# A hybrid decoder trunk: the attention gate on GpSimd, and each recurrent head's result turned one step later

## The chip, the cores and the metric

One core of a Trainium2 chip runs the whole program. The metric is device time in microseconds (us) of one execution; lower is better. The engines are TensorE (PE; its weight loads are listed as PEld), VectorE (DVE), ScalarE (ACT), GpSimd (POOL) and the queue of SyncE (SP). Each engine works through its own list of instructions in order and waits on semaphores; ACT, POOL and SP also issue DMAs.

## What is computed

Two layers over 1024 tokens of width 1024. Each layer normalises, projects, and runs two token mixers side by side: sliding-window attention and a gated linear recurrence (HGRN2). Both results are gated, projected up, merged, projected out and added to the input. Cut to what matters here:

```python
for layer in range(DEPTH):                       # 2
    h = rms_norm(x, norm_w[layer])
    (q, k, v, z_attn, q_h, f_h, i_h, g_h, gate_attn, gate_hgrn) = split(h @ w_in[layer])
    ...
    a = sliding_window_attention(q, k, v, sinks) * silu(z_attn)        # the gate of attention
    ...
    o = hgrn2_recurrence(heads(qin), heads(kin), heads(i_h), heads(logf))   # 4 heads of 128
    o = o * rsqrt(mean(o * o) + eps) * hgrn_norm_w[layer]
    b = o.reshape(B, T, 512) * silu(g_h)
    merged = sigmoid(gate_attn) * (a @ w_up_attn) + sigmoid(gate_hgrn) * (b @ w_up_hgrn)
    x = x + merged @ w_out[layer]
return rms_norm(x, final_norm_w)
```

All of it is float32. To keep that precision, the large products are made from operands that are each split into two parts of a narrower matmul type (fp32r): a high part, cast by ScalarE, and a low part, which is the operand less its high part. Three matmuls (low x high, high x low, high x high) stand for one.

## The kernel before

Tiles have 128 partitions. The names that matter:

- `slot(...)` hands out one of 39 SBUF buffers of 128 x 1024 floats; a load into a slot waits until the last reader of its former content is done. `bank(...)` hands out one of five PSUM banks, `pj` three more.
- `split_slot` (line 380) splits an operand: `S.copy` casts the high part on ScalarE (line 383), a subtraction makes the low part (line 384). `split_w` (136, 137) does the same for weights.
- `colsA` and `up` issue the projections, three matmuls a term through `proj3` (147 to 149).

The stage of a layer that the change touches is the heads. After attention, the four heads of the recurrence run as generators `core(h)` of ten steps each, one head started every five steps of a loop over `t`. A head's steps are these. Steps 0 and 1 load `f`, `R`, `Q` from DRAM (SP queue) and multiply them up on VectorE (`grow`, lines 946, 955, 958, and 967 to 975). Step 2 makes the first small score matmuls (`lv`, 933 and 992), which wait for those products. Steps 3 to 5 grow further, and step 6 makes the next score matmuls (`l`, `lv_m`, 1044 to 1057) and, in the step behind it, the masked scores are copied into `scT`, four pieces by GpSimd (1070). Then comes a turn of `R` (`tn`, 1080), and the state products (`kv`, 1092), which VectorE chains from chunk to chunk (1096, 1098). The last step makes the head's outputs (`po`, 1109 and 1111), copies them (1112) and sums their squares on ScalarE (1114), computes the reciprocal root on VectorE in small instructions (`ms_o`, lines 116 to 130) and scales the result (`tab`, 1116).

`finish_head` (1117 on) then turns the head's result: a load of its gate (`gg`, 1119), eight PE transposes (`tb`, 1125), a VectorE product with the norm's gain and the gate (`b`, 1126) and, for every second head, a split.

So that TensorE is not idle while a head's chain runs on other engines, the loop takes pieces of "filling" from a second generator: twelve halves of the projections of heads 1 to 3 (24 matmuls each; DVE subtracts the low part of their weights at line 137), then the up-projections of attention (`up_attn`, tiles `pu_ua`; 12, 12 and 24 matmuls a piece, twelve pieces). Between these, at the four pieces of `GATE = (6, 7, 8, 9)`, `gate_attn` loads a quarter of attention's output (`ar<-ad`) and of its gate (`zr<-zd`), multiplies them (line 1140) and splits the product (383, 384). The up-projections of attention read these splits; those of the recurrence (`pu_uh`), after the loop, read the splits of `b`.

The order within each engine's list is not simply the program's: the framework orders instructions when the program is built, by its own estimate of when each can start; where several can, the earlier in the program goes first. On the chip each list is then followed in that order.

## Time and profile before

| | |
|---|---|
| median of three runs | 1387.02 us (1384.45 to 1387.6) |
| the profiled execution | 1387.23 us, of which 1385.5 us lie between its first and last instruction |
| mean granted clock of TensorE | 0.996 |
| busy: PE, PEld, DVE, ACT, POOL | 98%, 81%, 72%, 51%, 8% of the span |
| the heads' stage | about 425 to 575 us in layer 0, 1119 to 1256 us in layer 1 |
| gate products (line 1140) | 8 on DVE, 1.22 us each |
| their low parts (line 384, `wl_a`) | 8 on DVE, 1.22 us each |
| the whole of POOL's other copies into `scT` | 32, 0.66 us each |

A row of the timeline gives start and duration in us, the engine, the line, the operation, the tiles (written <- read), shapes and count, and in brackets how long the engine idled before it and what released it. A row of waits gives who waited for whom, the total in us, how often, and the longest. A matmul of 512 columns is listed with 0.39 us because matmuls overlap; one starts every 0.23 us.

### The profile page before, as it was taken

The numbers are of one execution on the slowest core, as the hardware profiler recorded it, in microseconds if no ns is written. First come the engines' busy times: TensorE is split into PE (matmuls) and PEld (weight loads), VectorE is DVE, ScalarE is ACT, GpSimd is POOL, SyncE is SP. The second block draws the span as 40 slices with busy tenths as digits, with TensorE's granted clock in tenths as the row PEclk, the third lists the DMA queues.
The fourth block names the chain that finished last, engine by engine and source line by source line (L and its number), as shares of the span: only waits on it lengthen the run. The fifth ranks groups of instructions, "written<-read, shape, count | busy, mean of one in ns | idle before, by whom it ended". The sixth has DMA issues, their size and how long they took to land.

```text
span 1385.5 us, 21538 instructions
## 1 busy us (share of the span) xinstructions
PE 1356.9 (98%) x8236; PEld 1127.0 (81%) x8236; DVE 997.3 (72%) x1638; ACT 708.8 (51%) x1418; POOL 109.2 (8%) x195
## 2 busy tenths in 40 slices
PE   7999999999999999999999999999999999999997
PEld 7888888888877888888888888887887788788885
DVE  6867668843646898599959666776356487867998
ACT  8844333443786655323666333344367766352254
POOL 1100012320000001000000001222100000100000
PEclk9999999999999999999999999999999999999999
DMA  9444476875225652860256336587913476329203
GB/s 290 165 134 145 137 225 204 264 262 212 92 95 189 231 189 76 310 239 29 86 181 189 126 125 194 173 259 217 335 49 107 142 236 217 108 85 402 91 1 122
DMA packets 204279, 240.06 MB, mean 173 GB/s; under 512 B 14288, under 2 KB 140752, under 8 KB 204176
## 3 DMA queue, kind: packets, MB, share of 16 engines
q1 hardware_dynamic: 156528, 145.08, 32.0%
q10 hardware_dynamic: 34944, 52.44, 10.4%
q0 software_dynamic: 12704, 41.17, 9.3%
q8 instruction: 65, 1.06, 0.3%
q14 instruction: 38, 0.31, 0.1%
HBM read 160.00 MB, written 78.64 MB: 172 GB/s over the span
## 4 chain that ended last, share of the span: by engine, by line
PE 80%; DVE 13%; ACT 3%; DMA 2%; issue 2%; SPq 0%; DVEq 0%; ACTq 0%
PE pb L308 6%; PE pb L310 6%; PE pb L309 6%; PE pc L308 4%; PE pc L310 4%; PE pc L309 4%; PE pg L270 3%; PE pg L272 3%; PE pg L271 3%; PE pu_uh L149 2%; PE pu_uh L147 2%; PE pu_uh L148 2%; PE pi L843 2%; PE pi L842 2%; PE pi L844 2%; PE av L816 2%
## 5 line engine op out<-in xcount | busy, mean ns | idle before, releaser
L136 ACT CAST whi_s<-ws 128x1024 fp32r<-128x1024 f32 x30 | 31.6, 1054 | 90.4 <-PE pc L310 89.0
L319 DVE TENSOR_TENSOR pq<-pc,pq 128x512 f32<-128x512 f32 x37 | 25.6, 691 | 61.4 <-PE pc L310 56.2
L136 ACT CAST whi_o<-wo 128x1024 fp32r<-128x1024 f32 x20 | 21.1, 1054 | 78.7 <-PE pu_uh L149 35.5
L544 ACT ACTIVATE pq<-pq 128x512 f32<-128x512 f32 x60 | 37.9, 631 | 43.9 <-DVE pq L319 42.3
L136 ACT CAST whi_t<-ws 128x1024 fp32r<-128x1024 f32 x30 | 31.6, 1054 | 41.8 <-PE pc L310 27.9
L147 PE MATMUL pu_ua<-wh_a,wlo_ua 128*128 128x512 f32 x128 | 52.2, 408 | 0.0
L780 ACT ACTIVATE pr<-pr,mx 128x128 f32<-128x128 f32 x128 | 49.6, 391 | 4.1 <-DVE mx L777 3.7
L149 PE MATMUL pu_ua<-wh_a,whi_ua 128*128 128x512 f32 x128 | 51.0, 399 | 0.0
L148 PE MATMUL pu_ua<-wl_a,whi_ua 128*128 128x512 f32 x128 | 50.3, 393 | 0.0
L147 PE MATMUL pu_uh<-wh_b,wlo_uh 128*128 128x512 f32 x128 | 49.8, 389 | 0.0
L148 PE MATMUL pu_uh<-wl_b,whi_uh 128*128 128x512 f32 x128 | 49.8, 389 | 0.0
L149 PE MATMUL pu_uh<-wh_b,whi_uh 128*128 128x512 f32 x128 | 49.8, 389 | 0.0
L270 PE MATMUL pg<-hh,wl_p 128*128 128x512 f32 (+1 forms) x128 | 46.9, 368 | 1.0 <-DVE wl_p L384 1.0
L308 PE MATMUL pb<-th,wl 128*128 128x512 f32 x120 | 47.2, 393 | 0.5 <-ACT pq L349 0.4
L308 PE MATMUL pb<-th,wlo_s 128*128 128x512 f32 x120 | 47.1, 392 | 0.0
L308 PE MATMUL pc<-hh,wlo_t 128*128 128x512 f32 x120 | 46.8, 390 | 0.0
L310 PE MATMUL pb<-th,wh 128*128 128x512 f32 x120 | 46.7, 389 | 0.0
L309 PE MATMUL pb<-tl,wh 128*128 128x512 f32 x120 | 46.7, 389 | 0.0
L310 PE MATMUL pc<-hh,whi_t 128*128 128x512 f32 x120 | 46.7, 389 | 0.0
L309 PE MATMUL pc<-hl,whi_t 128*128 128x512 f32 x120 | 46.7, 389 | 0.0
L310 PE MATMUL pb<-th,whi_s 128*128 128x512 f32 x120 | 46.7, 389 | 0.0
L309 PE MATMUL pb<-tl,whi_s 128*128 128x512 f32 x120 | 46.7, 389 | 0.0
(432 smaller groups left out, 4447.4 us busy)
## 6 DMA issues: line engine op xcount, KB each, us to landing
wr<-in_w_in_dram SPq DMA_DIRECT2D x72, 512.0 KB, 4.6
gd<-pq ACTq DMA_DIRECT2D x79, 256.0 KB, 3.0
fq<-fq ACTq DMA_DIRECT2D x48, 256.0 KB, 2.7
wr_p<-in_w_in_dram SPq DMA_DIRECT2D x23, 512.0 KB, 5.6
x<-in_x_dram SPq DMA_DIRECT2D x16, 512.0 KB, 6.3
qs<-qsd POOLq DMA_DIRECT2D x16, 512.0 KB, 7.5
u<-gd SPq DMA_DIRECT2D x16, 512.0 KB, 10.1
ga<-gd SPq DMA_DIRECT2D x16, 512.0 KB, 10.3
```

Source lines behind the costliest of these rows:

```text
L136: S.copy(hi, raw)
L147: PE.matmul(acc, lhsT=ll, rhs=rh, start=i == 0, stop=False)
L148: PE.matmul(acc, lhsT=lh, rhs=rl, start=False, stop=False)
L149: PE.matmul(acc, lhsT=lh, rhs=rh, start=False, stop=i == n - 1)
L270: PE.matmul(acc, lhsT=wl[:, k], rhs=h[:, t], start=k == 0, stop=False, skip_group_check=q > 0)
L271: PE.matmul(acc, lhsT=wh[:, k], rhs=l[:, t], start=False, stop=False, skip_group_check=q > 0)
L272: PE.matmul(acc, lhsT=wh[:, k], rhs=h[:, t], start=False, stop=k % 4 == 3, skip_group_check=q > 0)
L308: PE.matmul(acc, lhsT=wl[:, k], rhs=h, start=start and k == 0, stop=False, skip_group_check=not start)
L309: PE.matmul(acc, lhsT=wh[:, k], rhs=l, start=False, stop=False, skip_group_check=not start)
L310: PE.matmul(acc, lhsT=wh[:, k], rhs=h, start=False, stop=k == 3, skip_group_check=not start)
L544: S.activation(d, src, AF.Sigmoid if r < 2 * KT else AF.Silu)
L780: S.activation(pr[:, h], pr[:, h], AF.Exp, bias=mx[:, h:h + 1], accum_out=sm[:, h:h + 1])
```

## The change

Two edits, for both layers:

1. `split_slot` takes an engine for its subtraction. In `gate_attn` the product and the subtraction are issued on GpSimd (`G`) instead of VectorE (`V`). The cast of the high part stays on ScalarE. The split of `b` keeps VectorE.
2. In the loop, `finish_head` of heads 0, 1 and 2 is issued at t = 12, 17 and 22 instead of 11, 16 and 21, each behind that step's piece of filling. For head 3, which is finished after the loop, one piece of filling is issued first.

```diff
-    def split_slot(raw, nm, shape):
+    def split_slot(raw, nm, shape, eng=V):
         hi = slot(shape, f"wh_{nm}", F32R)
         lo = slot(shape, f"wl_{nm}", F32R)
         S.copy(hi, raw)
-        V.tensor_tensor(out=lo, in0=raw, in1=hi.bitcast(F32), op=ALU.subtract)
+        eng.tensor_tensor(out=lo, in0=raw, in1=hi.bitcast(F32), op=ALU.subtract)
         return hi, lo
...
                 nc.sync.dma_start(d, src[:, 2 * j:2 * j + 2, a * 512:(a + 1) * 512])
-            V.tensor_tensor(out=t, in0=t, in1=zr, op=ALU.mult)
-            asp[a].append(split_slot(t, f"a{L}_{a}_{j}", [P, 2, 512]))
+            G.tensor_tensor(out=t, in0=t, in1=zr, op=ALU.mult)
+            asp[a].append(split_slot(t, f"a{L}_{a}_{j}", [P, 2, 512], G))
...
             if t % 5 != 4 or t < 12:
                 next(fill, None)
-            if t in (11, 16, 21):
+            if t in (12, 17, 22):
                 finish[done]()
                 done += 1
+        next(fill, None)
         finish[done]()
         for _ in fill:
             pass
```

## The prediction

> **What bounds the kernel now.** I read the page first: engine shares and the chain that ended last.

> ```profile
> PE 1356.9 (98%) x8236; PEld 1127.0 (81%) x8236; DVE 997.3 (72%) x1638; ACT 708.8 (51%) x1418; POOL 109.2 (8%) x195
> PE 80%; DVE 13%; ACT 3%; DMA 2%; issue 2%; SPq 0%; DVEq 0%; ACTq 0%
> ```

> PE is the bound over the whole, so time is won or lost only where PE waits. The change touches one stage of each layer, the heads. The waits on PE there, first layer 0 (420 to 580 us), then layer 1 (1120 to 1270), whose row for tb is the same as layer 0's:

> ```profile
> PE lv L992 <- DVE R L955: 2.1, 1, 2.1
> PE tb L1125 <- DVE tab L1116: 1.7, 3, 0.9
> ...
> PE lv L992 <- DVE R L955: 3.8, 1, 3.8
> ```

> Next the timeline of PE at those two lv waits (both of head 2), and the windows for the granted clock (the last three columns are clock, DMA share, GB/s):

> ```profile
> 501.38 0.64 PE L992 MATMUL lv<-f,ones 128*32 128x256 f32 x8 [2.07 <-DVE R L955]
> 505.60 1.72 PE L1092 MATMUL kv<-gs,f 128*128 128x128 f32 x14
> 1180.14 1.08 PE L992 MATMUL lv<-f,ones 128*32 128x256 f32 x8 [3.77 <-DVE R L955]
> 1186.87 1.72 PE L1092 MATMUL kv<-gs,f 128*128 128x128 f32 x14
> 1182.00:1184.00 2.00, 2.00 (x25) 1.06 (x15) 2.00 (x4) 0.63 (x3) 0.00 (x0) 0.50 0.11 20
> ```

> Layer 0 needs 4.22 us from lv to kv, layer 1 6.73 for the same work: after the 3.77 us wait the clock fell to 0.50, after the 2.07 us wait it did not. The lv waits thus cost 2.07 + 3.77 + 2.51 = 8.35 us, the tb waits 3.4. That is all that this change can win.

> **What the change moves off VectorE.** The groups of the gate's tiles, and DVE's busy time (third pair) in the gates' stretch and behind it, two stretches of layer 0 and the idle one of layer 1:

> ```profile
> L1140 DVE TENSOR_TENSOR ar<-ar,zr x8: 1215/1224/1254, 458.5 to 1162.4; 128x1024 f32<-128x1024 f32 x8
> L384 DVE TENSOR_TENSOR wl_a<-ar,wh_a x8: 1211/1221/1226, 461.4 to 1164.7; 128x1024 fp32r<-128x1024 f32 x8
> 463.00:477.00 14.00, 14.00 (x80) 12.19 (x79) 13.83 (x27) 8.94 (x15) 0.00 (x0) 1.00 0.43 146
> 477.70:483.50 5.80, 5.80 (x30) 4.75 (x28) 0.00 (x0) 5.19 (x18) 0.00 (x0) 1.00 1.00 330
> 1154.80:1162.30 7.50, 7.50 (x106) 6.24 (x109) 0.00 (x0) 5.32 (x18) 0.00 (x0) 1.00 0.96 314
> ```

> Four gates a layer, two instructions each: 8 x 1.22 = 9.8 us leave DVE. Up to 477 us DVE is full, then it idles until the fourth gate's data land.

> **What the eight cost on GpSimd.** Rows of DVE and POOL from the timeline:

> ```profile
> 11.02 2.73 POOL L137 TENSOR_TENSOR wlo_p<-wr_p,whi_p 128x1024 fp32r<-128x1024 f32 x1 [10.13 <-ACT whi_p L136]
> 10.32 1.22 DVE L137 TENSOR_TENSOR wlo_p<-wr_p,whi_p 128x1024 fp32r<-128x1024 f32 x1
> 547.67 0.39 POOL L1070 COPY scT<-acc 32x256 f32<-32x256 f32 x1 [23.18 <-DVE yt_o L129]
> 548.61 1.48 POOL L1070 COPY scT<-acc 32x256 f32<-32x256 f32 x1
> 548.61 1.23 DVE L1116 TENSOR_TENSOR tab<-tab,y_o 128x1024 f32<-128x1024 f32 x1
> 489.52 1.86 POOL L1070 COPY scT<-acc 32x256 f32<-32x256 f32 x4 [33.67 <-DVE y_o L130]
> 453.01 2.85 POOL L1070 COPY scT<-acc 32x256 f32<-32x256 f32 x4 [62.61 <-DVE acc L1067]
> 453.90 0.88 DVE L946 TENSOR_TENSOR Q<-Q,f 128x512 f32<-128x512 f32 x1
> 456.96 0.69 DVE L946 TENSOR_TENSOR Q<-Q,tab 128x512 f32<-128x512 f32 x1
> ```

> The copy of 0.39 us took 1.48 when it began with a DVE product of 1.23: it did its work after the product had ended. Conversely the DVE product of 0.69 takes 0.88 among four POOL copies, and the copies take 2.85 among DVE's long products instead of 1.86 among its short ones: the two take turns, one whole instruction at a time. The one subtraction of the gates' shape on POOL shows 2.73 us; of these DVE's own held it until 11.54, so its work is 13.75 - 11.54 = 2.2 us. So each gate instruction takes 1.22 us from DVE's queue and can hold a DVE instruction with two SBUF inputs for 2.2. Eight of them: -9.8 and up to +17.6 us a layer. What hides the holds is DVE's idle 5.8 to 7.5 us, and instructions that read PSUM. Queued behind the gates on POOL are only each head's four scT copies; head 1's come at 489.52 and their reader, po of head 1, is three steps of the loop away, so a gate in front of them costs nothing. Queued behind the cast on ACT are PSUM copies that PE waits for only through three buffers; the trace shows no PE wait on ACT here (the rows of waits above are all there are), so I price that at nothing while ACT stands for less than one piece of filling.

> [...]

> **Place 1, po of head 0, both layers.** The rows that make its slack:

> ```profile
> 457.57 0.69 DVE L955 TENSOR_TENSOR R<-R,tab 128x512 f32<-128x512 f32 x1
> 460.37 0.64 PE L992 MATMUL lv<-f,ones 128*32 128x256 f32 x8
> 476.11 0.34 DVE L1098 SCALAR_TENSOR_TENSOR R<-R,tab,kv 128x128 f32<-128x128 f32 x1
> 477.91 0.39 PE L1111 MATMUL po<-R,Q 128*128 128x128 f32 x2
> 461.48 0.37 SPq L873 DMA_DIRECT2D wr_ua<-in_w_up_attn_dram  x1
> ```

> Lv of head 1 has 2.1 us of slack, one hold: free or a few tenths. The last state that po reads is done at 476.45 and wanted at about 477.9: 1.4 us of slack. Ahead of it five gate instructions leave DVE (-6.1) and five holds may come (+11.0); about 1 us of them falls on PSUM-reading work. 11.0 - 6.1 - 1.0 - 1.4 = 2.5 us of new wait at the upper middle. If the third product lands behind that state (SP queues its loads behind wr_ua, which waits for a DVE subtraction that is itself held), four holds remain: 0.3. With every hold paid: 4. I take 2.0 a layer, nearer the row of a full DVE: **+4.0**.

> **Place 2, lv of head 2.** DVE's chain to it, the ACT cast that stands among head 0's squares, and the loads on SP:

> ```profile
> 483.59 1.23 DVE L1140 TENSOR_TENSOR ar<-ar,zr 128x1024 f32<-128x1024 f32 x1 [6.01 <-DMA ar<-ad]
> 483.17 0.31 ACT L1114 ACTIVATE f<-tab 128x128 f32<-128x128 f32 x1
> 484.85 1.05 ACT L383 CAST wh_a<-ar 128x1024 fp32r<-128x1024 f32 x1 [1.27 <-DVE ar L1140]
> 487.07 0.16 DVE L116 TENSOR_SCALAR ms_o<-so 128x8 f32<-128x8 f32 x1
> 493.51 1.21 DVE L967 TENSOR_TENSOR gs<-R,Q 128x1024 f32<-128x1024 f32 x1
> 1162.36 1.23 DVE L1140 TENSOR_TENSOR ar<-ar,zr 128x1024 f32<-128x1024 f32 x1 [7.62 <-DMA ar<-ad]
> 477.22 0.47 SPq L1139 DMA_DIRECT2D ar<-ad  x1
> ```

> DVE's root (487.07) follows the last square, and head 2's products follow the root by 6.4 us. If the cast moves behind the squares, the root starts near 484.5, 2.6 earlier (layer 1, 4.2: its products at 483.59 and 1162.36 lie 678.8 apart, the arrivals of PE at lv, 499.31 and 1176.37, only 677.1, so its data land 1.7 later). If it stays among them it waits for a product of 2.2 instead of 1.22 on POOL: 483.5 + 2.2 + 1.05 + 0.9 for the two squares left, each 0.31 and a read-out, = 487.6, 0.5 later. Middles: -1.0 and -1.9. The fourth gate's two holds are at most +4.4; half of them on work of no conflict: +2.2. Layer 0: +1.2, the wait becomes 3.3, still short of a fallen clock; layer 1: +0.3, clock loss unchanged. **+1.5**; ends -8.35 (both waits gone) and +4 a layer, with 2.5 for layer 0's clock. [...]

> **The turns one step later.** The same 32 transposes a layer (8 a head) are issued, with the same gg load on SP, behind one more piece. Two waits on tab in layer 0:

> ```profile
> 496.93 1.03 PE L1125 MATMUL tb<-ident,tab 128*128 128x128 f32 x8
> 528.29 1.06 PE L1125 MATMUL tb<-ident,tab 128*128 128x128 f32 x8 [0.87 <-DVE tab L1116]
> 529.19 1.04 PE L1080 MATMUL tn<-ident,R 128*128 128x128 f32 x8
> 571.88 1.06 PE L1125 MATMUL tb<-ident,tab 128*128 128x128 f32 x8 [0.68 <-DVE tab L1116]
> ```

> Head 1's turn now comes behind the next step's tn, which covers the 0.87: -0.9 a layer. A DVE product of b and its splits move with the turn, to a place where their readers, the up-projections of the hgrn branch, are still two pieces away. The 0.68 of head 3 stays, since filling already ran ahead of that turn. Head 0's waited for nothing; it covered 0.87 us ahead of lv, which I count in the ends. The later gg load and splits are hidden by the up-projections still to come; without these the splits are late for pu_uh. **-1.8**; ends -3.4 and +1.7.

> **Sum.** The profiled execution took 1387.23 us (span 1385.5 and 1.7 around it), 0.2 over the median of 1387.02. 1387.2 + 4.0 + 1.5 - 1.8 = 1390.9.

> **Rivals.**
> - *Faster: DVE is freed.* POOL's turns fall into DVE's idle stretch, and the root starts by 485.0 in layer 0, the point from which lv of head 2 no longer waits. For it: 9.8 us less on a chain that runs along DVE, and the idle 6 to 7.6 us that now only POOL waits through. Against: the gates land while DVE is full. Place 1 free, 8.35 and 1.8 won less about 3 of remaining holds: 1380.
> - *No change.* The holds lengthen DVE's work by what leaves it, place 1 stays inside its slack, and the lv waits stay: 1387.2.
> - *Slower, much.* ACT, in order, stands at a cast that waits for a held POOL product, and the squares, the root and both lv waits follow; layer 0's clock falls too. 4 x 2 at place 1, 2 x 2 at lv, 2.5: 1401.

> **How the numbers follow.** About 0.2% (2.8 us) is what a measurement of this kernel can tell from no change. Slower as summed 0.30, much slower 0.13, no change 0.22, faster 0.35. Both signs hold much, so the range reaches from 1379 to 1400; the likeliest case's own is 1389 to 1396. Faster 0.35, same 0.22, slower 0.43.

> **What would show it.** Right: eight POOL products and eight subtractions in the program, each 2.2 to 3.5 us; DVE rows of 0.69 near 457 to 477 stretched to 2 and more; a new PE wait at po on DVE R L1098 in both layers; lv of head 2 still waiting. Wrong: no stretched DVE rows, or stretched ones with no PE wait; the lv waits gone and the clock at 1.00 throughout layer 1's heads. DVE's busy time tells little, since a held instruction counts as busy.

## The result and the profile after

The changed kernel takes 1407.96 us (median of 4 runs, 1407.04 to 1408.22), the kernel before 1386.24 in the same comparison: a ratio of 1.0149, with a 95% interval of 1.0129 to 1.0169, or about 21 us more. The forecast was 1390.9, with a range of 1379 to 1400. (The ratios and intervals below are each against the kernel before, timed in the same comparison.) The profiled execution has a span of 1406.4 us against 1385.5, and a mean granted clock of 0.990 against 0.996.

The page of the changed kernel: engine shares, then the rows of its groups for what moved to GpSimd:

```profile
PE 1366.1 (97%) x8236; PEld 1133.0 (81%) x8236; DVE 1006.5 (72%) x1622; ACT 710.7 (51%) x1418; POOL 148.8 (11%) x211
```

```profile
L384 POOL TENSOR_TENSOR wl_a<-ar,wh_a 128x1024 fp32r<-128x1024 f32 x8 | 21.2, 2650 | 17.7 <-ACT wh_a L383 17.7
L1140 POOL TENSOR_TENSOR ar<-ar,zr 128x1024 f32<-128x1024 f32 x8 | 20.9, 2606 | 21.7 <-DMA ar<-ad 19.5 <-ACT whi L136 2.2
```

VectorE has 16 instructions less and is busy 9.2 us longer: a held instruction counts as busy. The waits of PE over the whole run, the rows that belong to the heads:

```profile
PE pu_ua L147 <- DVE wlo_ua L137: 6.4, 2, 3.8
PE po L1111 <- DVE R L1096: 6.3, 2, 3.3
PE lv L992 <- issue: 3.1, 2, 1.8
PE lv L992 <- ACT f L1081: 1.7, 2, 0.8
PE po L1111 <- DVE R L1098: 1.6, 2, 1.2
PE tb L1125 <- DVE tab L1116: 1.3, 2, 0.7
```

They sum to 20.4 us, against 9.2 before (lv 5.8, tb 3.4). Where the rest is shows when the stage is cut by the starts of PE's instructions. Stretch A runs from the first po of head 0 to the next projection, B from there to the first kv of head 2, C from there to the first up-projection of the recurrence:

```
             layer 0: A      B      C     layer 1: A      B      C
before            3.26   27.55  69.50         3.26   31.76  69.33
after             9.21   32.61  69.63         9.90   32.60  69.72
difference       +5.95   +5.06  +0.13        +6.64   +0.84  +0.39
```

A costs 12.6 us, B 5.9, C 0.5: 19.0 of the 20.9 us of span. Each figure is from one profiled execution. (Of the other 1.9, 1.4 are there before stretch A of layer 0 begins, and arise between 205 and 261 us, where the two kernels have the same work. B differs little in layer 1 because before it already held a wait of 3.77 us and the fallen clock behind it.)

**Stretch A.** The timeline of the changed kernel, layer 0: VectorE, then GpSimd, then PE, then the windows with the clock:

```profile
459.74 2.35 DVE L958 TENSOR_TENSOR tab<-acc 128x128 f32<-128x128 f32 x1
464.08 2.89 DVE L946 TENSOR_TENSOR Q<-Q,acc 128x512 f32<-128x512 f32 x1
466.90 2.88 DVE L955 TENSOR_TENSOR R<-R,acc 128x512 f32<-128x512 f32 x1
474.17 2.89 DVE L955 TENSOR_TENSOR R<-R,tab 128x512 f32<-128x512 f32 x1
476.97 2.84 DVE L946 TENSOR_TENSOR Q<-Q,tab 128x512 f32<-128x512 f32 x1
479.73 0.28 DVE L1096 COPY R<-kv 128x128 f32<-128x128 f32 x1
480.53 1.10 DVE L1098 SCALAR_TENSOR_TENSOR R<-R,tab,kv 128x128 f32<-128x128 f32 x3
481.55 2.36 DVE L137 TENSOR_TENSOR wlo<-wr,whi 128x1024 fp32r<-128x1024 f32 x1
483.83 0.33 DVE L1098 SCALAR_TENSOR_TENSOR R<-R,tab,kv 128x128 f32<-128x128 f32 x1
...
459.48 2.46 POOL L1140 TENSOR_TENSOR ar<-ar,zr 128x1024 f32<-128x1024 f32 x1 [2.18 <-ACT whi L136]
463.10 3.33 POOL L384 TENSOR_TENSOR wl_a<-ar,wh_a 128x1024 fp32r<-128x1024 f32 x1 [1.16 <-ACT wh_a L383]
466.39 2.83 POOL L1140 TENSOR_TENSOR ar<-ar,zr 128x1024 f32<-128x1024 f32 x1
473.56 2.94 POOL L384 TENSOR_TENSOR wl_a<-ar,wh_a 128x1024 fp32r<-128x1024 f32 x1 [4.34 <-ACT wh_a L383]
476.46 2.80 POOL L1140 TENSOR_TENSOR ar<-ar,zr 128x1024 f32<-128x1024 f32 x1
480.42 2.41 POOL L384 TENSOR_TENSOR wl_a<-ar,wh_a 128x1024 fp32r<-128x1024 f32 x1 [1.16 <-ACT wh_a L383]
...
480.07 0.49 PE L1111 MATMUL po<-R,Q 128*128 128x128 f32 x2 [3.31 <-DVE R L1096]
484.22 0.49 PE L1111 MATMUL po<-R,Q 128*128 128x128 f32 x2 [0.37 <-DVE R L1098]
...
480.00:482.00 2.00, 1.93 (x9) 1.67 (x10) 1.93 (x6) 1.97 (x3) 1.58 (x1) 0.62 0.00 0
482.00:484.00 2.00, 1.85 (x9) 1.55 (x8) 2.00 (x2) 2.00 (x4) 0.83 (x1) 0.53 0.02 4
```

Four VectorE products of 0.68 us (0.68 to 0.69 before) take 2.84 to 2.89 beside a gate instruction of GpSimd: some 2.2 us of standing each time. The three L1098 between 480.53 and 481.63 take 1.10 us beside GpSimd's subtraction of 480.42, and the next three, from 483.83 on, take 1.10 us with GpSimd idle: these read one of their two wide inputs from PSUM, and they were not stretched. PE waits 3.31 + 0.37 us for the states, and in between runs po at a clock near 0.55. That clock is not the rest of the 5.95 us. In layer 0 the end of the stretch is set by VectorE: po's last three pairs need the states made from 483.83 on, which stand behind `wlo` (481.55), itself held by GpSimd until 482.83. The fifth of the seven states is ready at 484.16, and PE takes it at 484.22; at full clock PE would have been there earlier and waited longer. In layer 1 the waits are 2.99 and 1.20, the fifth state is ready at about 1172.25, and there the clock of 0.50 does add about 1.0 us: from that state to the end PE takes 2.15 us, in layer 0, at full clock, 1.14.

**Stretch B.** ScalarE, VectorE's root, GpSimd's fourth product, the issues on SP, and PE:

```profile
486.12 0.31 ACT L1114 ACTIVATE f<-tab 128x128 f32<-128x128 f32 x1
493.94 1.05 ACT L383 CAST wh_a<-ar 128x1024 fp32r<-128x1024 f32 x1 [7.41 <-POOL ar L1140]
...
498.91 0.17 DVE L116 TENSOR_SCALAR ms_o<-so 128x8 f32<-128x8 f32 x1 [3.65 <-ACT f L1114]
...
491.53 2.38 POOL L1140 TENSOR_TENSOR ar<-ar,zr 128x1024 f32<-128x1024 f32 x1 [8.70 <-DMA ar<-ad]
...
483.94 0.37 SPq L873 DMA_DIRECT2D wr_ua<-in_w_up_attn_dram  x1
485.02 0.48 SPq L1139 DMA_DIRECT2D ar<-ad  x1
...
509.06 0.80 PE L147 MATMUL pu_ua<-wh_a,wlo_ua 128*128 128x512 f32 x1 [3.79 <-DVE wlo_ua L137]
511.57 1.08 PE L992 MATMUL lv<-f,ones 128*32 128x256 f32 x8 [1.29 <-issue]
517.97 1.73 PE L1092 MATMUL kv<-gs,f 128*128 128x128 f32 x14
```

Before, six of head 0's eight squares stood ahead of the fourth cast in ScalarE's list, and the cast stood 1.27 us. Now one square does, and the cast stands 7.41 us with seven squares queued behind it. The root starts 11.8 us later (498.91 against 487.07). Of this, 7.3 us is what PE itself was late when stretch B began; counted from there, the fourth gate's loads leave as before (0.3 us ahead of it, before 0.8), the cast begins 1.8 us later, and the root 4.5 us later, most of the rest being the five more squares that now stand behind the cast. The weights' low part for the up-projection comes behind the root in VectorE's list, and PE waits 3.79 us at pu_ua, where it never waited before, and 1.29 at lv, where it waited 2.07. That is 3.0 of the 5.06 us; the clock of 0.50, which lasts until 514.6 us, adds some 1.5 (an estimate: half of the 3.0 us from lv on).

### The profile page after: what moved, and what is told of

It is laid out like the page before. It is cut to its first block, busy times and chain, and to the rows that moved or that the text cites. A ratio compares the mean times of both kernels' runs of the same rounds, so it can differ in the third digit from the quotient of the medians.

```text
span 1406.4 us, 21567 instructions
## 1 busy us (share of the span) xinstructions
PE 1366.1 (97%) x8236; PEld 1133.0 (81%) x8236; DVE 1006.5 (72%) x1622; ACT 710.7 (51%) x1418; POOL 148.8 (11%) x211
## 3 DMA queue, kind: packets, MB, share of 16 engines
q8 instruction: 65, 1.06, 0.3%
## 5 line engine op out<-in xcount | busy, mean ns | idle before, releaser
L136 ACT CAST whi_s<-ws 128x1024 fp32r<-128x1024 f32 x30 | 31.6, 1054 | 90.0 <-PE pc L310 88.7
L136 ACT CAST whi_o<-wo 128x1024 fp32r<-128x1024 f32 x20 | 21.1, 1055 | 78.6 <-PE pu_uh L149 35.5
L946 DVE TENSOR_TENSOR Q<-Q,tab 128x512 f32<-128x512 f32 x40 | 33.9, 847 | 26.9 <-PE l L1044 26.7
L136 ACT CAST whi_t<-ws 128x1024 fp32r<-128x1024 f32 x30 | 31.6, 1054 | 41.8 <-PE pc L310 27.9
L308 PE MATMUL pb<-th,wlo_t 128*128 128x512 f32 x120 | 46.8, 390 | 0.0
L308 PE MATMUL pc<-th,wlo_s 128*128 128x512 f32 x120 | 46.7, 389 | 0.0
```

The lines of the kernel that those rows point to most:

```text
L136: S.copy(hi, raw)
L308: PE.matmul(acc, lhsT=wl[:, k], rhs=h, start=start and k == 0, stop=False, skip_group_check=not start)
L946: return [V.tensor_tensor(out=Qv[:, :, 1], in0=Qv[:, :, 1], in1=Fv[:, :, 0:1].broadcast_to([P, n, hh]), op=ALU.mult)]
```

## The experiments

Three theories went into the first runs. A, turns: GpSimd's gate instructions hold VectorE and make ScalarE's cast late. B, latency: a GpSimd product is merely ready later. C: the moved turns of the heads cost the time. D, the new order of VectorE's list, joins them from the run with extra reads on.

**Which edit.** One edit at a time:

```diff
 # gate only: the change, with
-            if t in (12, 17, 22):
+            if t in (11, 16, 21):
...
-        next(fill, None)
         finish[done]()
 # turns only: the kernel before, with the same lines the other way round
```

> Only the first edit: the gates' product and subtraction on GpSimd, the heads' turns where they were. Theory A (turns: while GpSimd works on a gate instruction of 2.4 us, a VectorE instruction with two SBUF inputs stands still; head 0's states come late for po, and ScalarE stands at a cast behind the held fourth product, so root, wlo_ua and lv of head 2 follow): 1404 to 1409, the same two new waits of about 3 us a layer on PE at po (on R, line 1096), the clock at 0.50 behind them. Theory B (latency: a GpSimd product is simply ready later, so ScalarE stands at the cast; nothing holds VectorE): also slower, 1392 to 1400, but no VectorE product of 0.69 us stretched. Theory C (the moved turns cost it): 1384 to 1389.

Measured 1408.13 us, ratio 1.0144 (1.0126 to 1.0161): all of the loss, and inside A's range.

> Only the second edit: the gates stay on VectorE, the heads' turns are one step later. Theories A and B: 1383 to 1388 (head 1's wait of 0.87 us at tb goes, at most 0.9 us a layer, if nothing else starts to wait). Theory C: 1397 to 1408.

Measured 1389.57, ratio 1.0008 (0.9993 to 1.0023): a little above the range of A and B, far below C's, and no change by its interval. C falls: the gates' move is all of the loss. The turns' move gives nothing either: head 1's tb wait goes, but a wait at lv of head 3 comes (1.46 us in layer 0).

**Which instruction.** From the gate alone, one of the two instructions is put back:

```diff
 # product only
-            asp[a].append(split_slot(t, f"a{L}_{a}_{j}", [P, 2, 512], G))
+            asp[a].append(split_slot(t, f"a{L}_{a}_{j}", [P, 2, 512]))
 # low part only
-            G.tensor_tensor(out=t, in0=t, in1=zr, op=ALU.mult)
+            V.tensor_tensor(out=t, in0=t, in1=zr, op=ALU.mult)
```

> Turns as before; the product on GpSimd, the subtraction on VectorE. Theory A: half of the holds (four a layer of 2.4 us), but the cast still waits for a GpSimd product: the larger part of the loss stays, 1393 to 1402. Theory B: all of the loss stays, 1404 to 1409, since the low parts have no reader for many us. No VectorE product stretched behind a subtraction in either.

> Turns as before; the product on VectorE, the subtraction on GpSimd. The cast then waits for VectorE as before. Theory A: four holds a layer are left, three of them while VectorE is full: 1388 to 1396, VectorE products of 0.69 us stretched to 2.9 behind each subtraction, and a wait at po. Theory B: nothing waits for a late low part: 1383 to 1387, no wait at po.

Measured 1397.71 (ratio 1.0070, 1.0049 to 1.0090) and 1391.03 (1.0025, 1.0012 to 1.0038). Both are as A says; under B the first would have cost all and the second nothing. Together they cost 13 us, the gate alone 20. Stretch A shows why: it grows by 4.00 and 2.22 us (layers 0 and 1) with the product alone and by 1.21 and 0.97 with the low part alone, but by 6.56 and 5.55 with both. A second hold finds the slack already used.

**Whether it is GpSimd's reads.** The gates stay on VectorE. Behind each of their eight instructions GpSimd does extra work that nobody waits for, once by reading, once by writing:

```diff
             V.tensor_tensor(out=t, in0=t, in1=zr, op=ALU.mult)
+            G.tensor_tensor(out=zr, in0=zr, in1=zr, op=ALU.mult)             # reads
             asp[a].append(split_slot(...))
+            hi = asp[a][-1][0].bitcast(F32)
+            G.tensor_tensor(out=zr, in0=hi, in1=hi, op=ALU.subtract)         # reads
 # the other run has, in place of each added product:
+            G.tensor_copy(zr[:, 0, 0:8], ...)
+            for _ in range(5):
+                G.memset(zr[:, 0], 0.0)                                      # writes
```

> The kernel before, its gates on VectorE and VectorE's list in its old order; behind each gate product and each gate subtraction GpSimd does one more instruction of the same size (128x1024, two SBUF inputs) that nobody waits for; it changes no result. Theory A (turns): every one of the eight a layer can hold a VectorE product for 2.4 us, and VectorE has kept its own work: 1398 to 1415, waits at po of head 0. Theory B (latency of the gates alone): nothing waits for these instructions, 1385 to 1389. Theory D (the new order of VectorE's list, not the holds, makes the states late): 1385 to 1389, since the order is the old one.

> The same places as the run with extra reads, but GpSimd writes instead of reading: a copy of 8 columns and five memsets of 512 columns each time, some 2.6 us of work without a wide read; it changes no result. Theory A with the hold tied to GpSimd's reads: 1385 to 1389, VectorE products of 0.69 us not stretched. Theory A with a hold by any GpSimd work, and power or clock as a rival: as slow as the run with reads, 1398 or more. Theory B and D: 1385 to 1389.

Measured 1406.81 (ratio 1.0146, 1.0122 to 1.0171) and 1387.71 (1.0005, 0.9991 to 1.0019). The same two VectorE products, with GpSimd beside them, first in the run with reads, then in the run with writes:

```profile
470.93 2.06 DVE L1023 TENSOR_TENSOR f<-Q,tab 128x256 f32<-128x256 f32 x1
472.91 2.11 DVE L1023 TENSOR_TENSOR gs<-Q,tab 128x256 f32<-128x256 f32 x1
...
470.81 1.89 POOL L1141 TENSOR_TENSOR zr<-zr 128x1024 f32<-128x1024 f32 x1 [5.90 <-issue]
472.78 1.96 POOL L1144 TENSOR_TENSOR zr<-wh_a 128x1024 f32<-128x1024 f32 x1
```

```profile
467.63 0.41 DVE L1023 TENSOR_TENSOR f<-Q,tab 128x256 f32<-128x256 f32 x1
467.96 0.42 DVE L1023 TENSOR_TENSOR gs<-Q,tab 128x256 f32<-128x256 f32 x1
...
467.75 2.86 POOL L1143 MEMSET zr<- 128x512 f32 x5
```

This is the clearest pair of the study: 2.06 and 2.11 us beside GpSimd reads, 0.41 and 0.42 beside GpSimd writes, for the same instructions at the same place in the same list. So in these two runs the VectorE products, whose two inputs are in SBUF, stood 1.65 and 1.69 us beside GpSimd instructions that read SBUF, and not at all beside those that only wrote. B and D are not needed for a loss of this size: in the run with reads nobody waits for GpSimd's results, and head 0's states keep their old places in VectorE's list. The added instructions also keep the buffer `zr` longer, but so do the writes (3.05 us each time), which cost nothing. In the run with reads stretch A is 8.63 and 8.69 us, and in layer 0 the clock stays at 1.00 all through it:

```profile
476.00:482.00 6.00, 3.71 (x21) 2.76 (x22) 6.00 (x13) 1.76 (x4) 0.34 (x1) 1.00 0.00 0
482.00:486.00 4.00, 3.32 (x17) 2.71 (x18) 3.76 (x3) 3.97 (x6) 3.92 (x2) 1.00 0.47 148
```

So the late states alone make A this long, without a fallen clock. D is tried by itself below.

**What freeing VectorE is worth.** This kernel leaves the gate out of the result altogether:

```diff
-            V.tensor_tensor(out=t, in0=t, in1=zr, op=ALU.mult)
-            asp[a].append(split_slot(t, f"a{L}_{a}_{j}", [P, 2, 512]))
+            hi = slot([P, 2, 512], f"wh_a{L}_{a}_{j}", F32R)
+            S.copy(hi, t)
+            asp[a].append((hi, hi))
```

> The gates' product and subtraction are left out on every engine: ScalarE casts the loaded attention output, and its cast stands for both parts. VectorE is rid of 9.8 us a layer, and GpSimd holds nothing. Theory A and B: the ceiling of what moving the gates could have won, 1376 to 1384, no wait at po, the wait at lv of head 2 mostly gone. Theory D: the waits at po stay, 1390 or more.

Measured 1380.59, ratio 0.9958 (0.9944 to 0.9971). With no gate product anywhere A stays at 3.26 us and B falls to 25.34 in both layers. So 6 to 7 us (0.42% by the ratio, 6.8 us between the medians) was about all that the move could have won, and the holds had to cost less than that.

**Which gates.** `E = G if ... else V` for both instructions, for the fourth gate alone (`a == 1 and j == 1`) and for the first three.

> Turns as before; only the fourth gate of each layer on GpSimd, the first three on VectorE. Theory A: place 1 is free of holds, so no wait at po; the cast of the fourth gate stands 1.2 us longer on ScalarE and the root with it: lv of head 2 waits about a us longer a layer, 1386 to 1391. Theory B (latency alone): the fourth gate is the one whose cast stands in front of the squares, so most of the loss stays: 1396 to 1406.

> Turns as before; the first three gates of each layer on GpSimd, the fourth on VectorE. Theory A: the holds of place 1 alone: both po waits of head 0 stay (about 3 us a layer and the clock behind them), and most of the 20 us, 1397 to 1403, so that this run and the run with the fourth alone (+6) add up to about the whole. If place 1 matters only by what it does to the fourth gate (its loads and ScalarE's cast): 1387 to 1392.

Measured 1393.62 (ratio 1.0051, 1.0033 to 1.0068) and 1403.74 (1.0135, 1.0120 to 1.0150). The fourth alone misses both ranges, a little above A's. Its row on ScalarE in layer 0 and its wait on PE in layer 1:

```profile
486.53 1.05 ACT L383 CAST wh_a<-ar 128x1024 fp32r<-128x1024 f32 x1 [2.56 <-POOL ar L1141]
```

```profile
PE lv L992 <- issue: 5.8, 1, 5.8
```

A GpSimd product 1.2 us longer and one square more behind the cast go with a wait of 5.8 us at lv of head 2 in place of 3.77 (the cast of layer 1 stands 4.56 us, before 2.88). The first three alone lie just above A's range too, and show both places again: A is 8.88 and 7.83, B 31.21 and 32.08. The two runs cost 7 and 19 us, more together than the gate's 20, so they do not add up as expected: with the first three alone the fourth cast, though its product is on VectorE, again stands ahead of seven squares (6.29 us).

**What makes stretch A dear: the holds, or the order of VectorE's list?** In the changed kernel the framework also put three more of head 1's products ahead of head 0's first state (479.73 above; before, 469.94 us), two of them the held ones of 474.17 and 476.97. This run forces the old order there, by order alone, without a wait:

```diff
+    behind = lambda ins, other: tc.add_manual_dep(..., DependencyClass.NoSync, ...)
...
             grown = grow(32)
+            # head 1's last four products, each behind one of head 0's first four states
+            [behind(i, states[0][k]) for k, i in enumerate((r16, q16, grown[1], grown[0])) if h == 1]
```

> The gates on GpSimd, turns as before, and VectorE's list held to the order of the kernel before in one place: head 1's last four products of steps 4 and 5 stand between head 0's states again, not ahead of them. Nothing else is changed. If the order is what made place 1 dear: the first state is no longer behind held products, the po waits of about 3 us and the clock behind them go, 1390 to 1398. If the holds alone do it: the same waits, 1404 to 1409.

Measured 1397.24, ratio 1.0065 (1.0046 to 1.0085): inside the range given for "the order". But the waits say otherwise. Layer 0 and then layer 1 of that run, and its issues on SP and the cast:

```profile
PE po L1111 <- DVE R L1098: 4.5, 2, 2.6
...
PE po L1111 <- DVE R L1098: 3.8, 2, 2.3
```

```profile
470.80 0.41 SPq L1139 DMA_DIRECT2D ar<-ad  x1
484.47 0.37 SPq L873 DMA_DIRECT2D wr_ua<-in_w_up_attn_dram  x1
...
487.19 1.03 ACT L383 CAST wh_a<-ar 128x1024 fp32r<-128x1024 f32 x1
```

The first state is early again, and po now waits for a later one: A stays at 9.29 and 9.58 us (9.82 and 8.81 with the gate alone). What fell is B, to 27.32 and 26.53, by 4.1 and 7.1 us. With the forced order the framework also changed SP's list: the fourth gate's loads are issued ahead of a load of wr_ua, which waits for a buffer until the held wlo is done. They leave at 470.8 in place of 484.9 us, and the cast stands for nobody although it is still behind only one square. So the holds make A dear in either order, as the run with reads also shows. For B this run shows that the cast's new place costs little once the fourth gate's data are early. The loads stood behind wr_ua before the change too (476.25 and 477.22 us), so what the change added in B is the longer product and the cast's place ahead of seven squares. SP's order and the cast's place were not varied one at a time; the split of B between them stays open.

**Whether another place for the gates helps.** `GATE` is changed, on GpSimd and on VectorE, and alone except where the text of a run says more:

```diff
-GATE = (6, 7, 8, 9)
+GATE = (7, 8, 9, 10)      # also (4, 5, 6, 7), (6, 7, 8, 10), (8, 9, 10, 11), (9, 10, 11, 12)
```

> The gates on GpSimd, turns as before, each gate one piece of filling later (7 to 10). Theory A: the third and fourth gate's holds leave the full stretch and the cast no longer stands in front of head 0's squares; the first two gates still hold: 1388 to 1398. If the place does not matter: 1404 to 1409.

Measured 1407.71 (ratio 1.0142, 1.0125 to 1.0158): a miss for A's range and inside that of "the place does not matter". GpSimd's third product still began at 476.56 us, so A stays at 9.69 and 8.82.

> The gates on GpSimd, turns as before, head 0's states put first in VectorE's list as in the run before, and each gate two pieces later (8 to 11). If order and place together take away what the holds cost: 1380 to 1387, no faster than the same places on VectorE (1380.2). If holds ahead of head 0's states remain: a wait at po of 1 to 3 us a layer, 1387 to 1397.

Measured 1396.28 (1.0072, 1.0057 to 1.0087). This is inside the second range, though po waits only 0.7 to 0.8 us a layer. With one gate fewer ahead of the states A falls to 5.00 and 5.31. The time is still 16 us above the same places on VectorE, which follow; most of that lies in B (30.82 and 30.66), where PE waits 3.7 us at lv_n for a copy on ScalarE.

> All gates on VectorE, each two pieces of filling earlier (4 to 7). Theory A: the fourth cast stands ahead of head 0's squares, the root starts near 484.5 us and lv of head 2 waits less, but more gates fall into the stretch in which VectorE is full: 1380 to 1388. If the stretch in which VectorE is full decides: slower, 1388 to 1394.

> The kernel before with all gates on VectorE; only the fourth gate is issued behind piece 10 of filling instead of 9. Theory A (the root of head 0 waits on ScalarE for the squares behind the fourth cast): the cast falls behind the squares, the root starts near 484.5 instead of 487.07 us, lv of head 2 waits less: 1380 to 1385. If the loads of head 2 or VectorE's list set lv instead: 1386 to 1389.

> All gates on VectorE, each one piece of filling later (7 to 10). Theory A: as with the fourth alone later, and one gate less in front of head 0's states: 1379 to 1385. If VectorE's list sets lv: 1386 to 1390.

> The gates on VectorE, each two pieces later (8 to 11). Theory A: one more gate leaves the full stretch, and no wait at lv of head 2: 1379 to 1384. If the up-projections of attention come to wait for the last gate: 1384 to 1395, with a PE wait at pu_ua.

> The gates on VectorE, each three pieces later (9 to 12). If the full stretch is still what costs: 1378 to 1380. If the up-projections of attention now wait for the last gates (loads of about 6 us and three instructions of 1.0 to 1.2 us behind piece 12): 1382 to 1395, with a PE wait at pu_ua.

> The gates on VectorE, one piece later (7 to 10), and the heads' turns one step later, as in the change. If the turns' move is worth what its covered waits show once nothing else waits: 1379 to 1382, that is 1 to 3 below the same gates with the old turns. If the move only trades a wait at tb for one at lv, as the run with the turns alone showed: 1381 to 1385.

Measured, in that order:

- (4, 5, 6, 7): 1394.07 (ratio 1.0068, 1.0050 to 1.0087), slower as the full stretch would have it, with a new wait of 4.2 us a layer at pj_f on wlo.
- (6, 7, 8, 10): 1386.94 (1.0011, 1.0001 to 1.0020), a miss for A. By its time it is in the other range, but the wait at lv of head 2 did go; C grew by 2.5 us a layer instead.
- (7, 8, 9, 10): 1382.59 (0.9980, 0.9971 to 0.9989), as A says.
- (8, 9, 10, 11): 1380.20 (0.9946, 0.9926 to 0.9965), as A says.
- (9, 10, 11, 12): 1386.01 (0.9999, 0.9987 to 1.0010), inside the second range, but not by its wait.
- (7, 8, 9, 10) with the moved turns: 1383.78 (0.9969, 0.9957 to 0.9981), the move only trades one wait for another.

The best one keeps the gates on VectorE, two pieces later. Its PE waits in the two stages:

```profile
PE tb L1125 <- DVE tab L1116: 2.3, 3, 1.1
...
PE tb L1125 <- DVE tab L1116: 2.0, 3, 1.1
```

Nothing else waits there: A is 3.26 and B 25.36 in both layers, as with the gates left out. One piece further C grows to 72.24 and 73.76 and takes it back; the wait expected at pu_ua did not come, but po of head 1 waits 1.2 and 2.7 us for its states. The moved turns on top of (7 to 10) gain nothing (1383.78 against 1382.59).

## Why the prediction was wrong, point by point

**Direction and mechanism: right.** Slower had the larger chance in sum (0.43), and the turns of the two engines were read correctly from four rows of before. The rival "slower, much" (1401, chance 0.13) described most of what came: po late, ScalarE standing at the cast, squares and root behind it. What failed are sizes: places 1 and 2 were summed at 5.5 us and measured 18.5.

**The hold, 2.2 us: about right.** Lone GpSimd instructions took 2.38 us; the VectorE products stood 2.2 us each.

**Place 1, +2.0 a layer: the step that failed first.** It measured +5.95 and +6.64. The step took 1.0 us off for holds that fall on PSUM-reading work, counted five holds, and then went below its own upper middle of 2.5. Of the six stretched rows none reads PSUM. The five before the states lost 2.1 to 2.2 us each, 10.8 in all where up to 11.0 was reckoned; the sixth, `wlo`, lost another 1.1 us. With all six and no deduction the step's own sum is 12.0 - 6.1 - 1.4 = 4.5 (with five it is 3.5, which the prediction writes as 4). The rest, 1.5 us in layer 0, fits its slack: it was taken at the last state, but in the new list `wlo` stands ahead of the last three, and PE still has three pairs of po to do (1.14 us) when the first of these is ready. In layer 1 another 1.0 us or so is the clock, which the step did not price.

**Place 2, +1.5: mis-sized, and its alternatives were incomplete.** B measured +5.06 and +0.84, with the turns in it. The step asked whether the cast would move behind the squares or stay among them. The list moved it ahead of seven. It stands there in every run at these places that has the product, the subtraction or both of the first three gates on GpSimd, and in none that keeps them on VectorE (five or six squares ahead); that this comes from the framework's estimates of when each instruction can start is our reading, and no run shows it. The pricing "at nothing while ACT stands for less than one piece of filling" did not apply: ACT stood 7.41 us, a piece being 5.6. The step also took a wait of 3.3 us to be too short for the clock to fall. No run shows such a limit: the clock fell to 0.50 behind waits of 1.93, 2.99 and 3.31 us and stayed at 1.00 behind one of 3.80 us (last section).

**The turns, -1.8: wrong.** The wait of 0.87 at tb went; PE then waits 0.8 at lv of head 3, for a copy of tn on ScalarE. Alone the move measured +0.08% (-0.07 to +0.23%).

**"Faster: VectorE is freed", chance 0.35: too much.** Its 1380 is what the run without gates reached, but only with no holds at all.

## What to carry to other kernels

Before an instruction moves to GpSimd, list the VectorE instructions with two SBUF inputs that run in the same microseconds and charge each GpSimd read in full (here some 2.2 us beside a gate instruction of 128x1024) against the smallest slack behind them; where VectorE is full, there is no idle time to hide a hold in. Where a planner orders the lists, look at every engine's new list, and look first for a better time for the work on the engine that it is on: here two pieces later was worth 0.5%, and the move of engine cost 1.5%. Before a loss is put down to a slow clock, look for what ends the stretch: in layer 0 the clock fell to half, and the stretch still ended when VectorE did.

## What the runs showed of the hardware that was not expected

The length of a wait on PE did not decide alone whether the clock falls. In the changed kernel it fell to 0.50 behind waits of 2.99 us (layer 1, at po) and 3.31 us (layer 0). It fell behind one of 1.93 us in the run with the first three gates (layer 1, at po), and stayed at 1.00 behind one of 3.80 us in the run with the fourth gate alone:

```profile
503.32 0.64 PE L992 MATMUL lv<-f,ones 128*32 128x256 f32 x8 [3.80 <-issue]
```

```profile
1161.71:1165.12 3.41, 1.48 (x10) 1.17 (x9) 3.41 (x4) 2.56 (x3) 2.38 (x1) 1.00 0.20 77
1165.12:1168.53 3.41, 3.41 (x16) 3.16 (x15) 3.34 (x5) 3.38 (x6) 2.41 (x1) 0.50 0.00 0
...
497.86:501.27 3.41, 1.67 (x16) 1.43 (x14) 3.38 (x5) 2.46 (x4) 0.00 (x0) 1.00 0.39 114
501.27:504.69 3.42, 1.37 (x80) 1.21 (x84) 3.39 (x7) 0.00 (x0) 0.00 (x0) 1.00 0.35 121
```

The wait of 1.93 us lies within one step, together with smaller gaps; PE is busy 1.48 us of it, and the clock is 0.50 in the next. The wait of 3.80 us is cut by an edge, and PE is busy 1.67 and 1.37 us on its two sides. No sharp limit comes out of the rows, since 1.37 us was enough here and 1.48 there was not. Nor was PE idle throughout the step ahead of a fall in any of these five. That where a wait happens to lie on the grid decides in part what it costs fits the two rows of each run and is the author's reading; no run moved a wait against the grid with all else the same. The fall in layer 1 of the kernel before cost 2.51 us, so a B or C that differs by 2 or 3 us between two single profiles may differ by one fall alone (an estimate from that figure).
